# A never-taken branch moved ahead of the second expert pass, and eight modulation steps moved forward at two places of a two-block network

## The chip, the core and the metric

The kernel runs on one core of a Trainium2 chip, in one launch. The metric is device microseconds (us) of that core, the median of the runs shown. The engines are TensorE (PE, matmuls; PEld its weight loads), VectorE (DVE), ScalarE (ACT), GpSimd (POOL) and SyncE (SP), which issues the weight loads. A "q" behind an engine's name is its instruction queue.

## The reference, cut to what matters

Two blocks of two layers each work on 256 tokens of width 1024, all in float32. In the first block a layer is a mixer and a mixture of 16 experts, each behind a norm whose scale and shift come from a small vector `c` through a large matrix; the second block is attention and an MLP, with scales and shifts made in the same way from `c_2` and `c_ctx_2`.

```python
def first_block(x, c, mod_w, mod_b, ...):
    cond = jax.nn.silu(c)
    for layer in range(DEPTH):
        mod = cond @ mod_w[layer] + mod_b[layer]
        sh1, sc1, g1, sh2, sc2, g2 = [m[:, None, :] for m in jnp.split(mod, 6, axis=-1)]
        h = rms_norm(x, mix_norm_g[layer]) * (1 + sc1) + sh1
        ...
        x = x + g1 * mix
        h = rms_norm(x, ffn_norm_g[layer]) * (1 + sc2) + sh2
        ffn = moe(...)
        x = x + g2 * ffn
    return x

def moe(h2, router_w, router_b, w1, w3, w2):
    ...
        y = (jax.nn.silu(xb @ w1[e]) * (xb @ w3[e])) @ w2[e]
        return y * g[:, None]

def second_block(x, c, ctx, c_ctx, w_mod, b_mod, ...):
    for l in range(DEPTH):
        mod = jax.nn.silu(c) @ w_mod[l] + b_mod[l]
        mod_c = jax.nn.silu(c_ctx) @ w_mod[l] + b_mod[l]
        ...
        h = x * (1 + sc1) + sh1
        hc = xc * (1 + sc1c) + sh1c
        y, yc = _token_mixers(h, hc, ...)
        x = _layer_norm(DEEPNORM_ALPHA * x + g1 * y, ln1_g[l], ln1_b[l])
        h = x * (1 + sc2) + sh2
        x = _layer_norm(DEEPNORM_ALPHA * x + g2 * _sq_relu_mlp(h, w_fc1[l], w_fc2[l]), ...)
        ...
```

## The kernel before, in words

`body` runs the phases one after the other: the first mixer (to 200 us), the experts of layer 0 (`moe(0)`, to about 465), the second mixer (`odd_mixer`, to about 583), the experts of layer 1 (to about 866), and block 2, per layer attention (`mixer2`), `out2` and `mlp2`. Activations lie transposed, 128 channels on the partitions by 256 tokens (512 where the context runs along). Weights are float32, split into a high part (`wh`, ScalarE, L332) and a low part (`wl`, VectorE, L325) and multiplied in three products (`linear`, L344 to L346).

**Weights.** `load` (L321) takes the next of a ring of buffers `raw` and issues the transfer from SP's queue. SP works in order: a load whose buffer is still read holds back all that stand behind it. The ring has 11 buffers of 512 KB in the mixers, 9 of 1 MB in the expert stages and 6 of 512 KB in block 2.

**Experts.** `moe` sends the tokens to 16 experts by one-hot products. The experts run in 7 passes over experts with limited room (PASSES: [8..11], [0], [2, 3], [4, 5], [1], [6, 7], [12..15]); `prep` builds a group of passes' inputs (L933) and gates, `up_` multiplies by w1 and w3 (four tiles of 1 MB per expert, L959 into `psab`), applies silu (`sa`, L973), transposes it (L976) and copies it out (`at`, L978); `down` multiplies by w2 (two tiles per expert, L959 into `psY`); `combine` adds the result to `xT` (L1000, L1002). The order of the tiles is up(0), up(1), down(0), up(2), down(1) and so on, 96 tiles per layer.

**Overflow.** Where an expert has more tokens than its room, `overflow` (L797 to L859) computes the rest; its body stands under `tc.If(n > 0)` (L804). With these inputs n is 0, so TensorE, ScalarE, VectorE and GpSimd load n into a register (L802) and branch over the body, about 355 rows of TensorE's program. `new_block` sets a dependency point on ScalarE behind it. Both stand behind `down` of pass 4, ahead of the last pass's `up_`, with the ring filled ahead (`fetch`).

**Modulation steps.** The vectors `mod` are made in groups of 1024 columns: ("a", l, g) for the first block, ("b", l, g) for the second. A group is eight steps (`unit`, L371 to L422): a step loads 128 rows of the matrix (512 KB; in the expert stages two steps share a 1 MB buffer) and multiplies it on TensorE by four products (L406); where `onv` holds an entry when the group begins, VectorE does it in four operations (L391, L393) instead. The eighth step copies the sums, transposes them (L417) and adds the bias (L420). All steps stand in one list, `queue`, in the order of the groups; `fill(n)` issues the next n, `settle` those that finish a group begun, `need` all up to a named group. `fill` does nothing in block 2's attention phases unless told `anyway`. The place of a step in the program is where `fill` stands, and the queue is taken in order, so a `fill` more at one place is a `fill` less later.

**The places around the change.** `odd_mixer` begins with the norm (`norm_split`, L465 to L519) and two linears of eight chunks with a `fill(1)` behind each. `mixer2` of layer 0 begins with the modulation of both streams (`modulate`: `hm`, L1117 or L1115, then its high part `h` on ScalarE, L340, and its low part on VectorE or POOL, L325), and then the chunks `ka`, `qa` with a `fill(1, True)` behind each. In `out2` a `fill(1)` follows each output chunk, and `need` of the groups ("b", 0, 3) and ("b", 0, 4) stands behind the first stream's last; in the first quarter of `mlp2` a step is issued behind a chunk while the queue holds more than 44.

Of the kernel before, what the change touches and what calls it, by code (L numbers as in the profile page):

```python
# [14 lines left out]
AF = mybir.ActivationFunctionType  # L15
# [186 lines left out]
def body(tc, A, out, co, po):  # L202
# [3 lines left out]
    with ExitStack() as ctx:  # L206
# [57 lines left out]
        def Pv(n, a=None, b=None):  # L264
# [10 lines left out]
        sets = {AF.Exp: "natural_log_exp_and_others", AF.Ln: "natural_log_exp_and_others",  # L275
                AF.Silu: "silu_and_others", AF.Sigmoid: "sigmoid_and_others", AF.Tanh: "sigmoid_and_others",
                AF.Gelu_apprx_tanh: "gelu_apprx_tanh_and_others", AF.Sqrt: "sqrt_and_others"}
# [3 lines left out]
        def tables(want):  # L281
            if table["set"] != want:
                before = table["users"] or [table["load"]] * bool(table["load"])
                ld = SC.preload_act_table_set(want)
                tc.keep_in_program_order(ld)
                ld = ld.ins
                for u in before:
                    tc.add_manual_dep(ld, u, nosync, reason="table order")
                table.update(set=want, load=ld.name, users=[])
# [8 lines left out]
        def new_block():  # L298

            t = sm.tile([128, 1], F32, tag="pin", bufs=2, name="pin")  # L300
            table.update(load=SC.copy(t, xT[:, 0, 0:1]).ins.name, users=[])
# [4 lines left out]
        KINDS = {"long": (11, 1024, 4), "wide": (9, 2048, 0), "short": (6, 1024, 3)}  # L306
# [121 lines left out]
        queue, onv = [], []  # L428
# [5 lines left out]
        def fill(n, anyway=False):  # L434
            if "M" not in banks and "ab" not in banks and not anyway:
                return
            for _ in range(min(n, len(queue))):
                queue.pop(0)[1]()
# [422 lines left out]
        def moe(l):  # L861
# [7 lines left out]
            gt, slot, gr, sr, idi, cap, mxc = router(hf, rs, m1(l, 3))  # L869
# [4 lines left out]
            th = [[U(F32R, "th", 4) for _ in range(2)] for _ in range(2)]  # L874
            tl = [[U(F32R, "tl", 4) for _ in range(2)] for _ in range(2)]
# [23 lines left out]
            def fetch(n):  # L899

                while len(ahead) < n:
                    w, r, j = next(todo_w, (None, 0, 0))
                    if w is None:
                        break
                    ahead.append((load(w[l][expert(r), j].rearrange("o p a n -> p (o a n)"), None, 2048), landing[0]))
# [6 lines left out]
            NP = len(PASSES)  # L912
            todo_w = sources()
            wide = lambda p: 128 // len(PASSES[p])
# [50 lines left out]
            def up_(p, pr):  # L965
                xg, _, gs = pr
                oa, ob = ps("ab"), ps("ab")
                for o in (oa, ob):
                    for j in range(2):
                        tiles(p, taken(p), [(o, xg[:, 4 * j + q, :], q * 512, j + q == 0, j + q == 4) for q in range(4)])  # L970
                sa = U(name="sa", bufs=2)
                func(sa, oa, AF.Silu)
                V.scalar_tensor_tensor(sa, sa, gs, ob, op0=OP.mult, op1=OP.mult)  # L973
                o = ps("X")
                for k in range(4):
                    T.transpose(o[:, 128 * k:128 * k + 128], sa[:, 128 * k:128 * k + 128], C("ident"))  # L976
                at = U(name="at", bufs=2)
                V.tensor_copy(at, o)  # L978
                return at
# [26 lines left out]
            for p in range(NP + 1):  # L1006
                if p < NP:
                    at[p] = up_(p, pr[p])
                if p:
                    todo.append((pr[p - 1][1], down(p - 1, at.pop(p - 1))))  # L1010
                    if len(todo) == 2 or p == NP:
                        combine(todo)
                        todo = []
                if groups and GROUPS[groups[0]][0] == p + 2:
                    pr.update(prep(groups.pop(0)))
                if p == NP - 2:
                    fetch(KINDS["wide"][0])
                    tables(sets[AF.Exp])
                    overflow(l, th, tl, gt, slot, cap, mxc)
                    new_block()  # L1020
            tables(sets[AF.Exp])


# [20 lines left out]
            V.tensor_scalar(nclam, clam, -1.0, None, op0=OP.mult)  # L1044

        def odd_mixer():
            assert not any(q[0] in (("a", 1, 0), ("a", 1, 1)) for q in queue)
            hh, hl = Act(8, S, F32R, "hh"), Act(8, S, F32R, "hl")
            norm_split(xT, 1, hh, hl)
            xc, r, ix, u = Act(8, name="xc"), Act(8, name="r"), Act(8, name="ix"), Act(8, name="uu")  # L1050
            y = Act(8, name="sq")
            w = Pv("cv_w").rearrange("p (a b) -> p a b", a=8)
            gw = [[U(name="gw", bufs=4) for _ in range(2)] for _ in range(2)]
            for q in range(2):
                for h in range(2):
                    SY.dma_start(out=gw[q][h].rearrange("p (a b) -> p a b", a=4), in_=A["od_gate"][:, q, 4 * h:4 * h + 4])
            for s in range(8):
                o = ps()
                linear(A["od_in"][8 + s], hh, hl, o[:, :S])
                V.tensor_scalar(xc(s), o[:, :S], w[:, s, 3:4], Pv("cv_b")[:, s:s + 1], op0=OP.mult, op1=OP.add)  # L1060
                for t in range(1, 4):
                    V.scalar_tensor_tensor(xc(s, t), o[:, :S - t], w[:, s, 3 - t:4 - t], xc(s, t), op0=OP.mult, op1=OP.add)
                fill(1)
            for s in range(8):
                o = ps("G")
                c = slice(s % 4 * 128, s % 4 * 128 + 128)
                T.matmul(o[:, :S], lhsT=gw[0][s // 4][:, c], rhs=xc(s), start=True, stop=True)
                T.matmul(o[:, S:], lhsT=gw[1][s // 4][:, c], rhs=xc(s), start=True, stop=True)
                func(r(s), o[:, :S], AF.Sigmoid, bias=Pv("rg_b")[:, s:s + 1])
                func(ix(s), o[:, S:], AF.Sigmoid, bias=Pv("ig_b")[:, s:s + 1])  # L1070
                func(u(s), r(s), AF.Tanh, scale=nclam[:, s:s + 1])
                G.tensor_mul(ix(s), ix(s), xc(s))

            for s in range(8):
                func(r(s), r(s), AF.Exp, scale=clam[:, s:s + 1])
                t = K1("t1")
                func(t, u(s), AF.Ln, bias=1.0)
                func(u(s), u(s), AF.Ln, scale=2.0)
                V.tensor_sub(u(s), u(s), t)
                func(u(s), u(s), AF.Exp, scale=0.5)  # L1080
                G.tensor_mul(ix(s), ix(s), u(s))
                V.tensor_tensor_scan(xc(s), r(s), ix(s), 0.0, op0=OP.mult, op1=OP.add)
            ch, cl = Act(8, S, F32R, "cath"), Act(8, S, F32R, "catl")
            for s in range(8):
                o = ps()
                linear(A["od_in"][s], hh, hl, o[:, :S], 0)
                V.tensor_copy(y(s), o[:, :S])
                fill(1)
            for s in range(8):
                func(y(s), y(s), AF.Gelu_apprx_tanh)  # L1090
                V.tensor_mul(y(s), y(s), xc(s))
                split(ch(s), cl(s), y(s))
            out_proj(A["od_out"], ch, cl, 1)
# [193 lines left out]
        def mixer2(l, bp, hs):  # L1287
# [2 lines left out]
            assert not any(q[0] in (("b", l, 0), ("b", l, 1)) for q in queue)  # L1290
            if l == 0:
                hs = Act(8, 512, F32R, "h", 16, bp), Act(8, 512, F32R, "h", 16, bp)
                for k in range(8):
                    for s in (1, 0):
                        modulate(l, 0, *hs, s, bp, (k,))
# [108 lines left out]

            qn, kn = f"qn{l}", f"kn{l}"
            if l == 0:
                onv.append(1)
                ka = chunk(2, 512)
                qa = [chunk(j, TQ) for j in range(2)]
                vab = values()  # L1410
                kb_ = chunk(5, 512, kn)
                qb_ = [chunk(3 + j, TQ, qn) for j in range(2)]
                settle(True)
                onv.clear()
                attend_ab(qa, ka, 0)
                ckv = low_k()
                cqh, cql = low_q()
                kc = rotary_k()
            else:
                qa = [chunk(j, TQ) for j in range(2)]  # L1420
                qb_ = [chunk(3 + j, TQ, qn) for j in range(2)]
                cqh, cql = low_q()
                ka = chunk(2, 512)
                vab = values()
                kb_ = chunk(5, 512, kn)
                attend_ab(qa, ka, 0)
                ckv = low_k()
                kc = rotary_k()
# [188 lines left out]
```

## Time and profile before

| | |
|---|---|
| median of 3 runs | 1956.85 us (1954.48 to 1958.96) |
| profiled execution | 1955.22 us |
| its span, first to last instruction | 1953.4 us |
| mean granted TensorE clock | 0.959 |
| TensorE busy | 1758.2 us (90%) |
| VectorE busy | 1078.6 us (55%) |
| ScalarE busy | 741.2 us (38%) |
| read from HBM | 437.35 MB |

A busy share is a mean over stages with different limits: in the expert stages the weight stream sets the pace, in block 2 mostly TensorE. A timeline row begins with its start and its length in us; a bracket at its end gives the idle time of the engine before it and what ended it. Windows give the busy time of each engine in a stretch.

### The profile page before, as it was taken

To read this page: it belongs to the slowest core of one execution; us is meant where nothing else is said; L and a number is where in the kernel's file an instruction comes from. 1 tells how busy PE (TensorE), PEld (TensorE's weight loads), DVE (VectorE), ACT (ScalarE), POOL (GpSimd) and SP (SyncE) were. 2 spreads that over 40 slices of the span, in tenths; PEclk is the share of its full clock that TensorE was granted. 3 is DMA by queue.
4 is the path that set the end of the run, shared out by engine and by line. 5 is a ranking of instruction groups with operands and counts; after the bars stand their busy time and mean duration, and the time that the engine had idled before them with its cause. 6 is when DMAs were issued, how large, how long until landed. Compare 5 with 4: busy or idle time off the path is not lost. (4 is left out here: it accounts for less than half of the span.)

```text
span 1953.4 us, 29087 instructions
## 1 busy us (share of the span) xinstructions
PE 1758.2 (90%) x11198; PEld 1256.4 (64%) x11198; DVE 1078.6 (55%) x2298; ACT 741.2 (38%) x1461; POOL 70.7 (4%) x88
## 2 busy tenths in 40 slices
PE   5999689967897799689999999999999999989997
PEld 4866234414783344237655779888888786669996
DVE  4987212104654112048778367678855767666665
ACT  3556100003642000124767355232323656544443
POOL 0000000000200000000010001000000200010000
PEclk8999899978998999889999999999999999989999
DMA  9685999997649999984100675555543220245551
GB/s 378 242 285 193 382 413 419 371 381 311 242 164 369 417 423 380 386 343 156 35 21 33 218 253 188 176 172 187 188 129 130 97 93 22 76 153 182 183 184 44
DMA packets 94361, 440.46 MB, mean 225 GB/s; under 512 B 10240, under 2 KB 10368, under 8 KB 69376
## 3 DMA queue, kind: packets, MB, share of 16 engines
q1 hardware_dynamic: 94208, 438.44, 60.0%
q8 instruction: 93, 1.52, 0.3%
q14 instruction: 60, 0.49, 0.1%
HBM read 437.35 MB, written 1.05 MB: 224 GB/s over the span
## 5 line engine op out<-in xcount | busy, mean ns | idle before, releaser
L332 ACT CAST wh<-raw 128x1024 fp32r<-128x1024 f32 (+1 forms) x258 | 261.4, 1016 | 281.8 <-PE psL L346 209.8
L325 DVE TENSOR_TENSOR wl<-raw,wh 128x1024 fp32r<-128x1024 f32 (+1 forms) x258 | 305.3, 1185 | 97.8 <-ACT wh L332 97.4
L959 PE MATMUL psab<-raw,xg 128*32 128x512 f32 (+2 forms) x1024 | 226.2, 705 | 76.1 <-DMA raw<-w 62.8
L344 PE MATMUL psL<-h,wh 128*128 128x256 f32 (+1 forms) x800 | 258.4, 323 | 7.6 <-ACT h L340 7.6
L345 PE MATMUL psL<-h,wl 128*128 128x256 f32 (+1 forms) x800 | 257.8, 323 | 4.0 <-DVE wl L325 3.9
L346 PE MATMUL psL<-h,wh 128*128 128x256 f32 (+1 forms) x800 | 256.4, 321 | 0.0
L959 PEld LDWEIGHTS psab<-raw,xg 128*32 128x32 f32 (+2 forms) x1024 | 73.9, 147 | 221.7 <-issue 193.7
L344 PE MATMUL psL<-gh,wh 128*128 128x256 f32 (+1 forms) x576 | 185.1, 322 | 0.0
L345 PE MATMUL psL<-gh,wl 128*128 128x256 f32 (+1 forms) x576 | 184.6, 321 | 0.0
L344 PEld LDWEIGHTS psL<-h,wh 128*128 128x128 f32 x800 | 154.2, 193 | 23.4 <-ACT h L340 8.3
L973 DVE SCALAR_TENSOR_TENSOR sa<-sa,gs,psab 128x512 f32<-128x512 f32 x14 | 10.5, 747 | 282.5 <-PE psab L959 282.5
L345 PEld LDWEIGHTS psL<-h,wl 128*128 128x128 f32 x800 | 154.2, 193 | 18.5 <-DVE wl L325 5.1
L346 PEld LDWEIGHTS psL<-h,wh 128*128 128x128 f32 x800 | 153.9, 193 | 14.2 <-issue 4.2
L959 PE MATMUL psY<-raw,at 128*32 128x512 f32 (+2 forms) x512 | 113.1, 611 | 9.3 <-DMA raw<-w 8.4
L346 PE MATMUL psL<-o,wh 128*128 128x256 f32 (+1 forms) x384 | 119.3, 311 | 0.3
L344 PEld LDWEIGHTS psL<-gh,wh 128*128 128x128 f32 x576 | 109.5, 190 | 14.5 <-issue 5.8
L345 PEld LDWEIGHTS psL<-gh,wl 128*128 128x128 f32 x576 | 109.5, 190 | 11.1 <-issue 3.7
L340 ACT CAST yh<-psY 128x512 fp32r<-128x512 f32 x28 | 16.4, 586 | 245.5 <-PE psY L959 245.5
L346 PE MATMUL psL<-gl,wh 128*128 128x256 f32 (+1 forms) x288 | 91.9, 319 | 0.0
L1525 ACT ACTIVATE t<-psL 128x256 f32<-128x256 f32 (+1 forms) x72 | 32.8, 456 | 139.1 <-PE psL L346 139.1
L1123 DVE SCALAR_TENSOR_TENSOR xT<-psL,mod2T,xT 128x256 f32<-128x256 f32 x80 | 38.6, 483 | 84.2 <-PE psL L346 84.0
L344 PE MATMUL psL<-hh,wh 128*128 128x256 f32 x256 | 77.8, 305 | 7.0 <-ACT hh L518 5.5
(449 smaller groups left out, 3340.9 us busy)
## 6 DMA issues: line engine op xcount, KB each, us to landing
raw<-w SPq DMA_DIRECT2D x192, 1024.0 KB, 11.7
raw<-fc SPq DMA_DIRECT2D x144, 512.0 KB, 3.5
raw<-mod_w SPq DMA_DIRECT2D x80, 512.0 KB, 6.6
raw<-w_mod SPq DMA_DIRECT2D x80, 512.0 KB, 3.9
raw<-wo SPq DMA_DIRECT2D x24, 512.0 KB, 4.7
raw<-wi SPq DMA_DIRECT2D x18, 512.0 KB, 3.3
raw<-ev_in SPq DMA_DIRECT2D x16, 512.0 KB, 7.4
raw<-mod_w SPq DMA_DIRECT2D x8, 1024.0 KB, 10.3
```

The costliest lines, as they stand in the source:

```text
L325: eng.tensor_sub(o, a, hi)
L332: SC.copy(hi[:, :w], raw[:, :w])
L340: SC.copy(hi, src)
L344: T.matmul(o, lhsT=wh, rhs=xh, start=start, stop=False)
L345: T.matmul(o, lhsT=wl, rhs=xh, start=False, stop=False)
L346: T.matmul(o, lhsT=wh, rhs=xl, start=False, stop=stop)
L959: r = T.matmul(o[w * i:w * i + w, :], lhsT=x[:, w * i:w * i + w], rhs=loads[i][0][:, c:c + 512], start=first, stop=last)
L973: V.scalar_tensor_tensor(sa, sa, gs, ob, op0=OP.mult, op1=OP.mult)
L1123: V.scalar_tensor_tensor(src2[s][:, n, :], o[:, s * S:s * S + S], mod2T[l][:, g, s, n:n + 1], src2[s][:, n, :], op0=OP.mult, op1=OP.add)
L1525: SC.activation(t[:, a:b], o[:, a:b], AF.Relu)
```

## The change

The block of `fetch`, `overflow` and `new_block` moves from behind pass 4 (`p == NP - 2`) to behind the `up_` of the first pass, in both expert stages. `odd_mixer` begins with `fill(8)`. `mixer2` of layer 0 issues eight steps ahead of the modulation, and the entry that puts the next group on VectorE goes in there too instead of ahead of `ka`. Nothing that is computed changes; the list of steps is only taken up earlier by eight at each of the two places.

```diff
@@ -1006,6 +1006,11 @@
             for p in range(NP + 1):
                 if p < NP:
                     at[p] = up_(p, pr[p])
+                if p == 0:
+                    fetch(KINDS["wide"][0])
+                    tables(sets[AF.Exp])
+                    overflow(l, th, tl, gt, slot, cap, mxc)
+                    new_block()
                 if p:
                     todo.append((pr[p - 1][1], down(p - 1, at.pop(p - 1))))
                     if len(todo) == 2 or p == NP:
@@ -1013,11 +1018,6 @@
                         todo = []
                 if groups and GROUPS[groups[0]][0] == p + 2:
                     pr.update(prep(groups.pop(0)))
-                if p == NP - 2:
-                    fetch(KINDS["wide"][0])
-                    tables(sets[AF.Exp])
-                    overflow(l, th, tl, gt, slot, cap, mxc)
-                    new_block()
             tables(sets[AF.Exp])
 
 
@@ -1044,6 +1044,7 @@
             V.tensor_scalar(nclam, clam, -1.0, None, op0=OP.mult)
 
         def odd_mixer():
+            fill(8)
             assert not any(q[0] in (("a", 1, 0), ("a", 1, 1)) for q in queue)
             hh, hl = Act(8, S, F32R, "hh"), Act(8, S, F32R, "hl")
             norm_split(xT, 1, hh, hl)
@@ -1290,6 +1291,8 @@
             assert not any(q[0] in (("b", l, 0), ("b", l, 1)) for q in queue)
             if l == 0:
                 hs = Act(8, 512, F32R, "h", 16, bp), Act(8, 512, F32R, "h", 16, bp)
+                fill(8, True)
+                onv.append(1)
                 for k in range(8):
                     for s in (1, 0):
                         modulate(l, 0, *hs, s, bp, (k,))
@@ -1404,7 +1407,6 @@
 
             qn, kn = f"qn{l}", f"kn{l}"
             if l == 0:
-                onv.append(1)
                 ka = chunk(2, 512)
                 qa = [chunk(j, TQ) for j in range(2)]
                 vab = values()
```

On TensorE the first pass and what follows it stand so in layer 0 before (psab<-raw,xg are products of `up_`, psX<-cst_108,sa the transposes of its result, psX<-P,th the preparation L933):

```order
774 L802 ISA x2
775 L959 MATMUL psab<-raw,xg 32x512 x64
776 L959 MATMUL psab<-raw,xg 128x512 x2
777 L976 MATMUL psX<-cst_108,sa 128x128 x4
778 L933 MATMUL psX<-P,th 128x256 x2
```

Behind the last of these stand the rest of the preparation, 14 more products of the second pass and the first down products. Now the branch follows the transposes, with the skipped body behind it:

```order
774 L802 ISA x2
775 L959 MATMUL psab<-raw,xg 32x512 x64
776 L976 MATMUL psX<-cst_108,sa 128x128 x4
777 L804 COMPARE_AND_BRANCH
778 L814 MATMUL psX<-cst_108,oP 128x128
```

Behind the body's end (row 1132) stand the 32 products L933, and then:

```order
1149 L941 MATMUL psX<-cst_108,P 128x128 x2
1150 L944 MATMUL psX<-rt,P 128x2 x2
1151 L941 MATMUL psX<-cst_108,P 128x128 x2
1152 L944 MATMUL psX<-rt,P 128x2 x2
1153 L959 MATMUL psab<-raw,xg 128x512 x16
1154 L959 MATMUL psY<-raw,at 32x512 x4
1155 L976 MATMUL psX<-cst_108,sa 128x128 x4
1156 L959 MATMUL psY<-raw,at 32x512 x28
```

All 16 products of the second pass stand behind the preparation, also the two that stood ahead of the transposes, and the branch stands between the transposes and the preparation. At the old place the compare and the body are gone.

On VectorE block 2 begins so before (hm and h are the modulation's, wl the low part of a weight, p the steps that VectorE does):

```order
883 L1117 TENSOR_SCALAR hm<-cT,mod2T_85 128x256
884 L1117 TENSOR_SCALAR hm<-xT,mod2T_85 128x256
885 L325 TENSOR_TENSOR wl<-raw,wh 128x1024
886 L325 TENSOR_TENSOR h<-hm,h 128x256 x2
887 L1117 TENSOR_SCALAR hm<-cT,mod2T_85 128x256
888 L1117 TENSOR_SCALAR hm<-xT,mod2T_85 128x256
889 L391 TENSOR_SCALAR p<-raw,cond_93 128x512 x2
890 L1117 TENSOR_SCALAR hm<-cT,mod2T_85 128x256
891 L1117 TENSOR_SCALAR hm<-xT,mod2T_85 128x256
892 L391 TENSOR_SCALAR p<-raw,cond_93 128x512
893 L325 TENSOR_TENSOR h<-hm,h 128x256 x2
894 L391 TENSOR_SCALAR p<-raw,cond_93 128x512
```

and now so (the lines of the changed kernel count one higher here):

```order
896 L1118 TENSOR_SCALAR hm<-cT,mod2T_85 128x256
897 L1118 TENSOR_SCALAR hm<-xT,mod2T_85 128x256
898 L1118 TENSOR_SCALAR hm<-cT,mod2T_85 128x256
899 L1118 TENSOR_SCALAR hm<-xT,mod2T_85 128x256
900 L325 TENSOR_TENSOR h<-hm,h 128x256 x2
901 L420 TENSOR_TENSOR mod2T_85<-psO,pv 128x8 x2
902 L325 TENSOR_TENSOR wl<-raw,wh 128x1024
903 L391 TENSOR_SCALAR p<-raw,cond_93 128x512 x4
904 L325 TENSOR_TENSOR wl<-raw,wh 128x1024
905 L393 SCALAR_TENSOR_TENSOR p<-raw,cond_93,p 128x512 x4
```

Ahead of these rows stand eleven more rows of hm and h alone: the whole chain of the modulation is now ahead of the first split and of the first step on VectorE, which stood among it.

On SP's queue block 2 begins so before (wi are the weights of the chunks, w_mod the steps'):

```order
537 L256 DMA cst<-cst 128x1536
538 L321 DMA raw<-wi 128x1024
539 L321 DMA raw<-w_mod 128x1024
540 L321 DMA raw<-wi 128x1024
541 L321 DMA raw<-w_mod 128x1024
542 L321 DMA raw<-wi 128x1024
```

and now so:

```order
538 L256 DMA cst<-cst 128x1536
539 L321 DMA raw<-w_mod 128x1024 x8
540 L321 DMA raw<-wi 128x1024
541 L321 DMA raw<-w_mod 128x1024
542 L321 DMA raw<-wi 128x1024
543 L321 DMA raw<-w_mod 128x1024
```

Eight loads of steps stand ahead of the first weight. In `odd_mixer`, likewise, eight loads raw<-mod_w stand ahead of those of the gates' weights (gw). In `out2` the run of nine loads raw<-w_mod ahead of one wo is gone, single loads alternate with wo.

## Rows read from the trace of the kernel before

**Rows 1.** The line of cores of the profiled execution.

```profile
core 0: 1953.4 us, clock 0.959
```

**Rows 2.** Windows: engines' busy us, PEclk, DMA share, GB/s; both expert stages.

```profile
275.00:280.00 5.00, 4.95 (x44) 1.74 (x36) 0.26 (x1) 0.60 (x2) 0.00 (x0) 1.00 0.88 305
...
390.00:395.00 5.00, 4.25 (x10) 1.52 (x8) 0.79 (x2) 1.28 (x3) 0.00 (x0) 1.00 1.01 421
...
400.00:405.00 5.00, 3.86 (x20) 1.25 (x24) 0.00 (x0) 1.48 (x2) 0.00 (x0) 0.50 0.82 339
405.00:410.00 5.00, 5.00 (x44) 1.51 (x40) 0.00 (x0) 0.00 (x0) 0.00 (x0) 0.83 0.28 79
...
805.00:810.00 5.00, 5.00 (x44) 1.45 (x40) 0.00 (x0) 0.00 (x0) 0.00 (x0) 0.90 0.23 59
```

**Rows 3.** Timeline of TensorE behind the branch's old place, layer 0: start, length, instructions.

```profile
401.14 9.37 PE L959 MATMUL psab<-raw,xg 128*32 128x512 f32 x60 [6.89 <-DVEq L804]
```

**Rows 4.** Instructions of line L804: ns min/median/max, first and last start.

```profile
L804 PEldq COMPARE_BRANCH  x2: 5812/5880/5949, 387.8 to 790.0; - x2
...
L804 DVEq COMPARE_BRANCH  x2: 63/68/72, 395.5 to 797.5; - x2
...
L804 DVEq EVENT_SEMAPHORE  x2: 21/21/21, 401.0 to 802.8; - x2
```

**Rows 5.** Timeline of TensorE around the new place, layer 0.

```profile
246.24 7.23 PE L959 MATMUL psab<-raw,xg 128*32 128x512 f32 x36 [4.67 <-DMA raw<-w]
...
253.66 0.48 PE L933 MATMUL psX<-P,th 128*128 128x256 f32 x2
...
258.78 12.26 PE L959 MATMUL psab<-raw,xg 128*128 128x512 f32 x28
...
272.55 7.40 PE L959 MATMUL psY<-raw,at 128*32 128x512 f32 x64
283.20 8.78 PE L959 MATMUL psab<-raw,xg 128*64 128x512 f32 x32 [3.25 <-DMA raw<-w]
```

**Rows 6.** Timeline of VectorE at the new place.

```profile
253.95 0.69 DVE L978 COPY at<-psX 128x512 f32<-128x512 f32 x1 [1.41 <-PE psX L976]
```

**Rows 7.** Windows at the second mixer's start, columns as in group 2.

```profile
460.00:465.00 5.00, 4.77 (x30) 2.02 (x21) 2.15 (x5) 2.46 (x3) 0.00 (x0) 0.87 0.00 0
...
480.00:485.00 5.00, 5.00 (x26) 5.00 (x25) 4.22 (x7) 1.84 (x3) 0.00 (x0) 0.50 1.02 419
```

**Rows 8.** Timeline of TensorE in the second mixer's first linear.

```profile
479.23 0.58 PE L345 MATMUL psL<-hh,wl 128*128 128x256 f32 x1 [1.32 <-DVE wl L325]
```

**Rows 9.** Timeline of VectorE at the start of block 2.

```profile
867.04 1.22 DVE L325 TENSOR_TENSOR wl<-raw,wh 128x1024 fp32r<-128x1024 f32 x1
```

**Rows 10.** Timeline of POOL there: the chain's last pair.

```profile
884.11 2.29 POOL L325 TENSOR_TENSOR h<-hm,h 128x256 fp32r<-128x256 f32 x2 [3.04 <-ACT h L340]
```

**Rows 11.** Timeline of TensorE there: the third chunk begins.

```profile
888.40 0.39 PE L344 MATMUL psS<-h,wh 128*128 128x512 f32 x1
888.63 0.39 PE L345 MATMUL psS<-h,wl 128*128 128x512 f32 x1
```

**Rows 12.** Windows behind it, columns as in group 2 (VectorE is the third).

```profile
900.00:910.00 10.00, 10.00 (x69) 9.24 (x68) 10.00 (x15) 3.12 (x5) 0.00 (x0) 1.00 0.75 243
910.00:930.00 20.00, 20.00 (x93) 14.18 (x91) 14.54 (x26) 11.34 (x18) 0.00 (x0) 1.00 0.35 118
```

**Rows 13.** Timeline of TensorE in out2: four modulation steps in a row.

```profile
1110.33 1.93 PE L406 MATMUL psM<-raw,cond2r 128*32 128x256 f32 x32
```

**Rows 14.** Timeline of SP's queue in out2.

```profile
1096.34 15.48 SPq L321 DMA_DIRECT2D raw<-w_mod  x9
```

**Rows 15.** Waits, 1065 to 1215 us: total us, times, longest.

```profile
ACT wh L332 <- DMA raw<-wo: 17.1, 6, 5.1
```

**Rows 16.** Windows in out2, columns as in group 2 (TensorE is the first).

```profile
1120.00:1125.00 5.00, 3.97 (x28) 3.27 (x27) 4.40 (x12) 3.99 (x8) 0.00 (x0) 1.00 1.01 391
1125.00:1130.00 5.00, 3.50 (x33) 2.33 (x33) 5.00 (x11) 4.51 (x9) 0.00 (x0) 1.00 0.78 257
```

## The prediction

> **What bounds the kernel now.** I read the line of cores first [rows 1]: span 1953.4 us, mean granted clock 0.959. The profiled execution took 1955.22 us, so 1.8 us lie around the span, and it stands 1.6 us under the median of the three runs, 1956.85. Every sum below is made against 1955.22; the 1.6 is added at the end. A measurement of this kernel can tell about 0.2%, 3.9 us, from no change.
>
> Next I read stretches of five microseconds around the old place of the branch, for DMA rate and clock. In the expert stages the weight stream runs at some 421 GB/s (390 to 395 us) [rows 2], and the layer ends when its 96 tiles of 1 MB are through and used, so a hole in this stream is lost unless TensorE was the later one anyway. Behind the branch there is such a hole in each layer: 339 GB/s and then 79 in layer 0, 59 in layer 1. TensorE's timeline shows why: the last pass's products (p = 6, experts 12 to 15) start at 401.14 after 6.89 us in which it waited for VectorE's queue at L804 [rows 3]. The rows of line L804 [rows 4] give the length of the skipped branch: VectorE's compare stands at 395.5 and the event that ends the region at 401.0; TensorE's own branch takes 5812 to 5949 ns.
>
> Then I read TensorE and VectorE at the new place [rows 5, 6], and last the places where the modulation steps are moved [rows 7 to 16].
>
> **Part 1: the branch moves ahead of the second pass.** What goes away: 5 x (1 - 339/421) + 5 x (1 - 79/421) = 1.0 + 4.1 = 5.1 us of stream in layer 0, and 5 x (1 - 59/421) = 4.3 us in layer 1 [rows 2], 9.4 us in all. The old TensorE stall was longer, 6.9 us, but nine loaded tiles stood ahead of it, and only what the stream lost counts.
>
> What comes instead: the order shows TensorE branching right behind the four transposes of the first pass, and VectorE right behind the copy of their result, with preparation of passes 2 and 3 (L933) behind. That copy ends at 253.95 + 0.69 = 254.64 [rows 6]. From compare to event VectorE took 5.5 us at the old place [rows 4]; with the compare at the end of that copy the event comes near 260.1, and L933, which now starts at 253.66 [rows 5], starts 6.5 us later. The two first products of the second pass, four records, filled the wait for the transposes before; now they follow the preparation: 4 x 12.26/28 = 1.75 us later [rows 5]. Against that, the transposes no longer stand behind them, about 0.75 us. After a pause of six microseconds the clock stood at 0.50 at the old place (400 to 405 us) [rows 2], and the next stretch had 0.83, so up to 2.7 us of work was lost; I take 2.0, since the preparation's short products need not all scale. That is 6.5 + 1.75 - 0.75 + 2.0 = 9.5 us.
>
> What could hide it is the wait for data on either side: TensorE waits 4.67 us for a tile before this place and 3.25 us after it, before the third pass at 283.20 [rows 5]. I do not count these as cover, because the ring has nine tiles: the tiles of the third pass go into the places that the first down products (272.55) release, and the DMA share falls to 0.88 at 275 to 280, with 305 GB/s [rows 2]. The stream is waiting for those releases already; a later release makes the third pass later by the same amount. Only the loss already there, 5 x (1 - 305/421) = 1.4 us, is not paid a second time. So 8.1 us per layer, 16.2 in two (layer 1 has the same order), and **part 1 is 16.2 - 9.4 = +6.8 us**. Its bounds are 0 per layer (all hidden in the two waits, -9.4 in all) and 9.5 (+9.6). I take the value near the upper one because of the ring, and for what I expect keep +2 to +9.6.
>
> [...]
>
> **Part 2: eight steps ahead of the second mixer's norm.** Each step is a 512 KB load and four products L406. In the order their loads stand ahead of the gate weights, where the DMA moves nothing (460 to 465 us, 0 GB/s) [rows 7]; 4 MB at 421 GB/s are 10 us and fit from where the experts' last tiles release their places. Their 32 products, 2 x 1.93 = 3.9 us by [rows 13], fall where TensorE waits for the norm. VectorE's order puts the eight pairs of the norm ahead of the first weight split, which now stands among them, so the first product L345 comes near 482.4 instead of 479.23 [rows 8], 3.2 us later. But TensorE ran at 0.50 from 480 to 485 [rows 7], after a pause that the 32 products now fill: at full clock 2.9 us from 482.4 do what was done by 485.2. **Part 2 is +0.5 us**; bounds +3.2 (clock as low as before) and -2 (first product no later, clock full).
>
> **Part 3: eight steps at the start of block 2.** Eight loads stand ahead of the first weight, 32 products ahead of the first linear on TensorE, and VectorE does the whole chain of `hm` and `h` before its first weight split. Before, that split was at 867.04 [rows 9] and the chain's last pair left POOL at 884.11 + 2.29 = 886.4 [rows 10]; both first chunks were through at 888.40, where the third starts [rows 11]. VectorE's part of the chain gets shorter without splits and steps: three splits of 1.22 us [rows 9] are 3.7 us of its time, and the steps L391 and L393 stood among them too; I give the chain 4.4 us, so that it ends near 882. With a split of 1.22 the first chunk runs from 883.3, 24 products, and the second, 24 more, behind it. One product follows the other in 0.23 us (888.40, 888.63) [rows 11], so both end near 894.4: 6 us later. VectorE's steps that were done among the chain now fall where it is full (10.00 of 10 us in 900 to 910) [rows 12], with 5.5 us free in 910 to 930; I add 1.5. **Part 3 is +7.5 us**; bounds +1 (the chain alone ends both) and +11 (chain no faster, more waits for splits).
>
> **Part 4: what is then missing later.** The queue is eight ahead after the mixer's norm and sixteen by block 2's second norm: 16 steps fewer in `out2` and the first quarter of `mlp2`. By [rows 13] four units are 1.93 us, so 16 are 7.7 us of TensorE. That engine is the bound there: in the two weakest stretches it is still busy 3.97 + 3.50 of 10 us [rows 16]. A run of nine loads stands ahead of an output weight in SP's queue there (15.48 us) [rows 14], ScalarE waits 17.1 us in six times for such weights [rows 15], and TensorE's 2.5 idle us of the two stretches come behind that run. I count 2.3 as saved. **Part 4 is -10 us**; bounds -12 and, where the waits stay and something else fills the gap, -2. What follows has the same steps as before.
>
> **Sum:** 6.8 + 0.5 + 7.5 - 10 = +4.8 us, 1960.0 for the profiled execution, 1961.6 on the median.
>
> **The rivals**, with times on the median. (a) *The pause is hidden at the new place*, which ends on the other side: TensorE waits 4.67 and 3.25 us for tiles there [rows 5], 7.9 in all, and if the stream is ahead by the length of the pause nothing is late. Part 1 is then -9.4, the sum -11.4, 1945. It decides from a cost under 3.8 us per layer, where the sum passes -3.9. For it speaks that these are true waits for data; against it the share of 0.88 at 275. Chance 0.12. (b) *The new start of block 2 hides behind the chain*: part 3 is +1, the sum -1.7, 1955. For it: VectorE is full in this stretch, and loses its splits and steps; against it, the one split now behind the chain. Chance 0.18. (c) *The branch costs the same in both places*, 4.7 us per layer: part 1 is 0, the sum -2.0, 1955. Chance 0.10. (d) *The relief doesn't arrive*: `out2` waits for weights and splits as before, part 4 is -2, the sum +12.8, 1970. Chance 0.15.
>
> **How the numbers follow.** My forecast has the remaining 0.45, by itself 1957 to 1966. Of it 0.02 is faster, 0.18 within 0.2% and 0.25 slower. (a) is faster, (b) and (c) give 0.11 faster and 0.17 within, (d) is slower with small rests: faster 0.25, same 0.33, slower 0.42. The range reaches from 1947, just over (a), to 1970, which takes in (d).
>
> **What would show it.** Part 1: no hole at 405; VectorE's event near 260 in layer 0; L933 a good six microseconds later; the third pass eight later. If the third pass starts under 287, (a) holds. Part 2: first L345 of the mixer 3 us later against the end of the experts, at full clock. Part 3: its third chunk 6 us or more later against the end of the experts; 1 us means (b). Part 4: that delay made good and 2 to 3 us more by 1220 us. A time under 1950 makes part 1 wrong, one over 1966 part 4.

## The result, and the profile after

The changed kernel takes 1974.26 us (median of 4 runs, 1971.96 to 1975.53) beside 1957.9 for the kernel before: ratio 1.0085, interval 1.0067 to 1.0102, so 16.6 us slower (13.1 to 20.0). The prediction had the sign, with +4.8 us, and a range that ended at 1970.

The line of cores of the profiled execution (1975.53 us) answers to [rows 1]:

```profile
core 0: 1973.8 us, clock 0.952
```

Windows of the changed kernel, columns as in [rows 2]. The first four lie behind the branch's new place in layer 0, the next two at the old place, the last two at the second mixer's start (they answer to [rows 7]):

```profile
255.00:260.00 5.00, 1.19 (x4) 1.14 (x5) 0.00 (x0) 0.19 (x1) 0.00 (x0) 0.52 1.01 421
260.00:265.00 5.00, 2.19 (x11) 2.19 (x11) 0.69 (x1) 0.00 (x0) 0.00 (x0) 0.50 1.00 415
265.00:270.00 5.00, 5.00 (x32) 5.00 (x31) 0.69 (x1) 1.52 (x3) 0.00 (x0) 0.62 0.22 90
270.00:275.00 5.00, 5.00 (x14) 2.35 (x14) 1.52 (x12) 1.66 (x2) 0.00 (x0) 1.00 0.16 23
405.00:410.00 5.00, 3.41 (x32) 0.78 (x24) 1.02 (x2) 0.46 (x1) 0.00 (x0) 1.00 1.01 426
410.00:415.00 5.00, 1.11 (x8) 0.45 (x12) 0.00 (x0) 0.00 (x0) 0.00 (x0) 0.72 1.02 433
480.00:485.00 5.00, 1.53 (x5) 1.21 (x5) 3.64 (x11) 3.93 (x8) 0.00 (x0) 0.55 1.02 419
485.00:490.00 5.00, 3.81 (x18) 3.81 (x19) 2.27 (x2) 2.08 (x3) 0.00 (x0) 0.50 0.89 329
```

The hole at the old place is gone: 426 and 433 GB/s. A larger one stands behind the new place, 90 and 23 GB/s: the ring's nine tiles were loaded, and SP waited for the products that free one, 21.0 us at the longest (waits from 255 to 290 us):

```profile
SPq L321 <- PE psab L959: 29.0, 4, 21.0
```

TensorE's timeline there (beside [rows 5]; left out are the transposes and the rest of the 32 products L933) shows why:

```profile
245.26 5.15 PE L959 MATMUL psab<-raw,xg 128*32 128x512 f32 x32 [4.86 <-DMA raw<-w]
...
258.19 0.76 PE L933 MATMUL psX<-P,th 128*128 128x256 f32 x2 [6.09 <-DVEq L804]
258.76 0.63 PE L933 MATMUL psX<-P,tl 128*128 128x256 f32 x2
262.81 0.59 PE L933 MATMUL psX<-P,th 128*128 128x256 f32 x2 [3.42 <-issue]
263.20 0.63 PE L933 MATMUL psX<-P,tl 128*128 128x256 f32 x2
263.62 0.63 PE L933 MATMUL psX<-P,th 128*128 128x256 f32 x2
...
269.99 13.98 PE L959 MATMUL psab<-raw,xg 128*128 128x512 f32 x32
...
293.40 3.65 PE L959 MATMUL psab<-raw,xg 128*64 128x512 f32 x16 [1.68 <-DMA raw<-w]
```

The pause of the branch is 6.09 us, close to the 6.5 of the forecast. But after four records (products, as the trace holds them) TensorE stands idle again, for 3.42 us, and for nothing the profile shows ("issue"). The rest of the preparation runs at the half clock (0.50, then 0.62 in the windows): one pair of products follows the other in 0.43 us, where it was 0.24 us in the kernel before. The third pass starts at 293.40. Two rows of the kernel before, for the pace:

```profile
254.22 0.40 PE L933 MATMUL psX<-P,th 128*128 128x256 f32 x2
254.46 0.40 PE L933 MATMUL psX<-P,tl 128*128 128x256 f32 x2
```

The waits of TensorE over the whole program sum this up (what waits <- for what: us, times, longest):

```profile
PE psX L933 <- DVEq L804: 12.2, 2, 6.1
...
PE psM L417 <- ACT mod_e L414: 8.0, 5, 5.6
...
PE psX L933 <- issue: 6.1, 2, 3.4
...
PE psO L417 <- ACT k L414: 5.6, 1, 5.6
```

The second idle stretch comes in both layers. And TensorE now waits twice for 5.6 us ahead of L417, once in each of the places that got eight steps.

From the timelines I read where the time went, with one profiled execution of each kernel: the expert stages run from the first product of `up_` to the end of the last of `down`, "between" lies between the two stages, "rest" behind the second. A second execution of the changed kernel differs by up to 2.6 us in a column, and layer 1 of the five kernels with the branch at its old place reads 242.3 to 245.7, so differences under some 3 us say nothing.

| kernel | layer 0 | between | layer 1 | rest | measured against before, us |
|---|---|---|---|---|---|
| before | 245.9 | 156.8 | 242.3 | 1091.4 | |
| the change | 250.5 | 161.8 | 253.0 | 1092.5 | +16.6 (13.1 to 20.0) |
| the change again | 251.4 | 162.5 | 250.4 | 1093.1 | +15.9 (11.0 to 20.8) |
| branch only | 251.5 | 156.9 | 246.4 | 1094.8 | +8.4 (4.9 to 11.8) |
| mixer steps only | 246.0 | 163.7 | 245.7 | 1087.4 | -3.7 (-6.5 to -1.0) |
| block 2 steps only | 245.2 | 157.6 | 245.2 | 1097.9 | +3.7 (1.0 to 6.7) |
| both steps | 245.5 | 162.6 | 243.7 | 1091.5 | +1.0 (-1.4 to 3.3) |
| no branch at all | 239.0 | 155.3 | 242.1 | 1092.0 | -4.5 (-7.8 to -1.4) |
| branch behind preparation | 246.1 | 155.7 | 246.5 | 1095.8 | +6.7 (3.9 to 9.4) |
| branch ahead of first pass | 235.4 | 163.5 | 233.8 | 1093.3 | -7.4 (-10.0 to -4.7) |
| the change, shifted by 8 products | 246.3 | 163.6 | 247.1 | 1095.4 | +11.0 (7.6 to 14.3) |
| mixer steps behind the gates | 244.0 | 171.9 | 243.4 | 1088.1 | +7.3 (4.5 to 10.0) |
| branch first, eight mixer steps | 235.8 | 166.7 | 236.1 | 1087.3 | -6.7 (-9.2 to -4.1) |
| branch first, four mixer steps | 236.4 | 173.2 | 236.4 | 1090.0 | -5.1 (-8.4 to -1.8) |

The last column is the measured ratio times the median of the kernel before in the same comparison (1957.9 to 1961.6). The profiled executions are single ones: those of before (1955.22) and without a branch (1949.07) lie 3 to 6 us below their medians, those of the mixer steps alone (1962.96) and of the last row (1961.14) 5 us above, so a row's sum and its last column differ.

### The profile page after: what moved, and what is told of

Same layout as the page of the kernel before. It is cut to its first block, busy times and chain, and to the rows that moved or that the text cites. A ratio compares the mean times of both kernels' runs of the same rounds, so it can differ in the third digit from the quotient of the medians.

```text
span 1973.8 us, 29087 instructions
## 1 busy us (share of the span) xinstructions
PE 1764.1 (89%) x11198; PEld 1261.1 (64%) x11198; DVE 1080.6 (55%) x2298; ACT 741.6 (38%) x1461; POOL 68.8 (3%) x88
## 3 DMA queue, kind: packets, MB, share of 16 engines
q8 instruction: 94, 1.54, 0.3%
## 5 line engine op out<-in xcount | busy, mean ns | idle before, releaser
L344 PE MATMUL psL<-h,wh 128*128 128x256 f32 (+1 forms) x800 | 256.9, 321 | 7.6 <-ACT h L340 7.6
L345 PE MATMUL psL<-h,wl 128*128 128x256 f32 (+1 forms) x800 | 257.7, 323 | 3.9 <-DVE wl L325 3.8
L344 PE MATMUL psL<-gh,wh 128*128 128x256 f32 (+1 forms) x576 | 185.1, 322 | 0.0
L345 PE MATMUL psL<-gh,wl 128*128 128x256 f32 (+1 forms) x576 | 184.6, 321 | 0.0
L344 PEld LDWEIGHTS psL<-h,wh 128*128 128x128 f32 x800 | 153.5, 192 | 22.4 <-ACT h L340 8.3
L345 PEld LDWEIGHTS psL<-h,wl 128*128 128x128 f32 x800 | 153.3, 192 | 20.1 <-issue 6.2
L973 DVE SCALAR_TENSOR_TENSOR sa<-sa,gs,psab 128x512 f32<-128x512 f32 x14 | 10.5, 748 | 277.2 <-PE psab L959 277.2
L344 PEld LDWEIGHTS psL<-gh,wh 128*128 128x128 f32 x576 | 109.5, 190 | 14.5 <-issue 5.8
L345 PEld LDWEIGHTS psL<-gh,wl 128*128 128x128 f32 x576 | 109.5, 190 | 11.2 <-issue 3.7
L393 DVE SCALAR_TENSOR_TENSOR sq<-raw,cond,sq 128x512 f32<-128x512 f32 x112 | 77.6, 746 | 11.1 <-DMA raw<-w_mod 11.1
L959 PEld LDWEIGHTS psY<-raw,at 128*32 128x32 f32 (+2 forms) x512 | 35.2, 132 | 72.3 <-issue 59.9
```

The costliest lines, as they stand in the source:

```text
L344: T.matmul(o, lhsT=wh, rhs=xh, start=start, stop=False)
L345: T.matmul(o, lhsT=wl, rhs=xh, start=False, stop=False)
L393: V.scalar_tensor_tensor(a, w, cols[1][:, i, k:k + 1], a, op0=OP.mult, op1=OP.add)
L959: r = T.matmul(o[w * i:w * i + w, :], lhsT=x[:, w * i:w * i + w], rhs=loads[i][0][:, c:c + 512], start=first, stop=last)
```

## The experiments

**The change taken apart.** Four kernels that each hold some hunks of the change's diff: the branch's move alone (its first two), `odd_mixer`'s alone (the third), block 2's alone (the last two), and both step moves.

```diff
+            fill(8)
...
+                fill(8, True)
+                onv.append(1)
...
-                onv.append(1)
```

> The kernel before with the branch alone moved behind the first pass's up products, in both layers; no step is moved. Theory A (the branch carries the loss: its pause is followed by an idle stretch of 2.6 to 3.4 us of TensorE for its own program and by products at half clock, and the stream's ring can't cover it): 13 to 16 us slower than before. Theory B (the branch costs what the prediction said, +6.8 us, and the moved steps carry the rest): 5 to 8 us slower.

> The kernel before with the eight steps ahead of the second mixer's norm alone. Theory A: the mixer's start is 3.4 us later and out2 has eight steps fewer, 3.9 us of TensorE: between -1 and +3 us. Theory B: +4 to +6 us.

> The kernel before with the eight steps at block 2's start alone. Theory A: the start is some 8 us later, eight steps fewer afterwards and no run of nine loads give 4 to 7 back: +1 to +4 us. Theory B: +4 to +6 us.

> Both step moves, the branch at its old place. Theory A: 1 to 5 us slower, and with the branch-only run it adds up to the 16 us of the whole change. Theory B: 9 to 11 us slower.

Measured +8.4, -3.7, +3.7 and +1.0 us. The branch alone lay between the two theories, with an interval (4.9 to 11.8) that takes in all of B; the steps spoke for A at block 2's start and together, and the mixer's steps alone came out below both. But +8.4 and +1.0 make 9.4, not 16: the pieces don't add up. The table shows where: in layer 1, 246.4 with the branch alone and 253.0 with everything. In the branch-only run TensorE's second idle stretch was there in one layer of two:

```profile
PE psX L933 <- DVEq L804: 12.5, 2, 6.3
PE psX L933 <- issue: 3.5, 1, 3.5
```

**Is it the place in the program?** Its timeline in layer 1 has no such stretch, and the products return to full pace after 4 us. Between the layers, the mixer's steps add 64 records of L406 and their weight loads to TensorE's program. So the next four kernels were the change again, no branch at all, and the branch at two other places.

> The changed kernel once more, beside the three below. Theory A (branch and steps add up, and the first measurement stands high): +9 to +11 us, as the branch alone (+8.4) and the steps alone (+1.0) make. Theory C (they don't add up: TensorE's second idle stretch behind the branch comes in both layers of the whole change and in one layer of the branch alone, and the moved steps shift TensorE's program between the two layers): +14 to +19 us, and the trace shows an idle stretch without a releaser behind the branch in both layers.

The ratio was 1.0081 (1.0056 to 1.0106), and the idle stretch came in both layers again (5.4 us in two times), behind the same number of records, 4 in layer 0 and 10 in layer 1. So the change costs more than its pieces; how much more is uncertain (by the intervals, an estimate, 2 to 12 us).

```diff
-                    overflow(l, th, tl, gt, slot, cap, mxc)
-                    new_block()
```

> The kernel before with the overflow left out altogether (with these inputs it is never entered), nothing else moved: the price of the old place. By the prediction's reading, the holes in the stream behind it are its price: 8 to 10 us faster. If the holes are made good later, 0 to 4 us faster.

The kernel without the branch was 4.5 us faster (1.4 to 7.8): the old place cost about half of what its holes in the stream, 9.4 us, had promised. In the traces most of it lies in layer 0, 239.0 us beside 244.0 to 246.0 in the five kernels with the branch at its old place; layer 1 has 242.1 beside 242.3 to 245.7.

```diff
-                if p == NP - 2:
+                if p == 0:
                     fetch(KINDS["wide"][0])
```

> The branch stands one place later than in the change: behind the preparation of passes 2 and 3, ahead of the second pass's products; no step is moved. Theory A (pause, idle stretch and half clock on the 32 short products make the loss): the preparation runs at full clock ahead of the branch, what follows are long products that need few instructions, no idle stretch: +2 to +5 us against before, 4 to 6 less than the branch alone. If the pause itself is the whole loss: as the branch alone, +7 to +10.

+6.7 us (3.9 to 9.4): between the two cases, and its interval reaches into both, so it doesn't tell them apart. It does show that, with the preparation done ahead and no idle stretch of 3 us behind, the pause (13.4 us in two times) still has a price, and the measured one is most of what the branch alone costs.

```diff
             for p in range(NP + 1):
+                if p == 0:
+                    fetch(KINDS["wide"][0])
+                    tables(sets[AF.Exp])
+                    overflow(l, th, tl, gt, slot, cap, mxc)
+                    new_block()
                 if p < NP:
```

> The branch stands ahead of the first pass's products; no step is moved. There TensorE waits for four groups of tiles, 16 us in sum, since the stream has only begun. Theory A (the place decides by what the stream has ahead): the pause delays the first release, the ring's nine tiles last until then, and the stream loses 0 to 3 us per layer instead of 4.7: -9 to -3 us against before. If a pause costs its full length anywhere (6 us per layer): +2 to +4.

-7.4 us. The same pause stands there, 6.94 us in layer 0:

```profile
222.04 3.59 PE L959 MATMUL psab<-raw,xg 128*32 128x512 f32 x11 [6.94 <-DVEq L804]
```

The stage begins some 5 us later, but is 10.5 and 8.5 us shorter: 235.4 and 233.8 us. The stream has only begun, and TensorE would have waited for tiles there anyway (from 215 to 260 us 16.0 us in four times before, 8.7 us in two here): in layer 0 the preparation L933 begins at 255.27, only 1.6 us later than before (253.66). With the branch here the kernel is no slower than without any (-4.5, intervals overlap).

**Eight products that do nothing.** At the very start of the whole change:

```diff
+                spare_o = ps("X")
+                for _ in range(8):
+                    T.matmul(spare_o[:, 0:1], lhsT=ones, rhs=ones[:, 0:1], start=True, stop=True)
```

> The whole change, with eight one-column products on TensorE put at the program's very start, 32 instructions, whose result nothing reads. They cost nothing there (TensorE waits for its first data) and shift everything behind by 32 places in TensorE's program. Theory C (the idle stretch behind the branch is TensorE waiting for the next piece of its program, which begins a few instructions behind the branch's end: after 4 products in layer 0, after 10 in layer 1): the shift puts the branch's end behind the start of that piece, the idle stretch is gone in both layers, the second pass starts 4 to 6 us earlier in each, and the whole is +4 to +10 us against before instead of +16. If the idle stretch has another cause (semaphores, data, the clock): it stays, and the time too, +14 to +19.

The idle stretch is gone in both layers, in the waits (no line L933 <- issue is left) and in the timeline of layer 0:

```profile
260.13 0.77 PE L933 MATMUL psX<-P,th 128*128 128x256 f32 x2 [6.39 <-DVEq L804]
260.69 0.63 PE L933 MATMUL psX<-P,tl 128*128 128x256 f32 x2
261.12 0.63 PE L933 MATMUL psX<-P,th 128*128 128x256 f32 x2
```

The order of all other products on TensorE is the same in the two traces, so the shift is what differs. The kernel takes 1971.11 us, 1.0056 (1.0039 to 1.0073), that is +11.0 us: some 5 of the 16 us came from where the branch's end falls in TensorE's program (by the intervals, an estimate, 1 to 10 us). Layer 0 is 246.3 instead of 250.5 and 251.4, layer 1 247.1 instead of 253.0 and 250.4. The second pass starts 4.5 us earlier in layer 0, as forecast, but in layer 1 only 2.6 and 0.8 us earlier than in the two executions of the change, where the transposes ahead of it also came 1.7 us later; the total came out just above the forecast of +4 to +10. From the first L933 to the second pass TensorE took 6.7 us here in layer 0 and 7.5 in layer 1, beside 11.8 and 11.5 (10.7 and 9.7 the second time) in the change:

```profile
266.87 13.98 PE L959 MATMUL psab<-raw,xg 128*128 128x512 f32 x32
```

**The mixer's steps at another place**, between the gates and the second linears of the same mixer:

```diff
+            fill(8)
             ch, cl = Act(8, S, F32R, "cath"), Act(8, S, F32R, "catl")
```

> The kernel before with the second mixer's eight steps at another place of the same mixer: behind the gates, ahead of its second linears, where TensorE stood idle for some 6 us; the branch and block 2's start are as before. If the steps' cost in the change is the mixer's later start (its first weights stand behind eight loads): the stretch between the two expert stages is 156 to 159 us in the trace instead of 162 to 164, and the kernel is 3 to 8 us faster than before. If eight steps cost the same wherever they stand in the mixer: as at its start, 162 and a total like that of the steps at its start alone (-3.7).

A miss: +7.3 us (4.5 to 10.0), with 171.9 us between the stages. TensorE's timeline names the reason:

```profile
530.15 1.02 PE L417 MATMUL psM<-cst,mod_e 128*128 128x8 f32 x4 [11.99 <-ACT mod_e L414]
```

The transposes of a group's end stand in TensorE's order ahead of the linears, and their input is copied by ScalarE, whose order has the copy behind a long chain. In the kernel before, products of these linears fill that time, from

```profile
510.83 0.47 PE L344 MATMUL psL<-hh,wh 128*128 128x256 f32 x1
```

on. Eight steps cost some 3.7 us of products (64 records L406), but where they end a group they tie TensorE to ScalarE's queue, here for 11.99 us.

**Combinations.** The branch ahead of the first pass, with eight and with four steps ahead of the mixer's norm (the two edits shown above, the second in its form for four):

```diff
         def odd_mixer():
+            fill(4)
```

> Two pieces that were faster alone: the branch ahead of the first pass (-7.4) and the eight steps ahead of the second mixer's norm (-3.7); block 2's start as before. If they add up: -14 to -8 us. If the moved program brings an idle stretch behind the branch here too, or the mixer's late start adds to the pause: -7 to 0.

> The branch ahead of the first pass, and four steps (not eight) ahead of the second mixer's norm: half a group, so that its transposes L417, which wait for ScalarE's copy behind the whole norm, no longer stand ahead of the first linear on TensorE. If that wait is what makes the mixer late (6 us with eight steps): the first L344 comes 10 to 12 us after the experts' last product instead of 16, the stretch between the expert stages is 2 to 4 us shorter than with eight steps (166.7 in that trace), and the total is -11 to -7 against before. If the loads ahead of the first weights make it late: the first L344 at 13, half of the delay, and a total like that of the branch ahead of the first pass with eight steps (-6.6) or without (-7.4).

With eight steps -6.7 us (-9.2 to -4.1), with four -5.1 (-8.4 to -1.8): nothing is gained beyond the branch's place. With four, "between" is 173.2 us, longer than the 166.7 with eight where 2 to 4 us less were expected; TensorE waits 8.37 us for a weight split within the second linears. The four-step kernel also refutes half of my reason. No L417 stands ahead of its first linear, and still the first L344 came 15.8 us after the experts' last product, because (first row; the second is the wait of 8.37)

```profile
478.50 0.58 PE L344 MATMUL psL<-hh,wh 128*128 128x256 f32 x1 [6.61 <-ACT wh L332]
...
533.78 0.58 PE L344 MATMUL psL<-hh,wh 128*128 128x256 f32 x1 [8.37 <-ACT wh L332]
```

ScalarE's first weight split stands behind all eight `hh` of the norm (476.61 is the last). In the kernel before, the first split (473.89) stood ahead of all `hh`. It is the order that ScalarE got with the steps ahead that delays the mixer, with or without the transposes.

The lowest ratio seen is that of the branch ahead of the first pass with no step moved: 1951.49 us (12 runs), 0.9962 (0.9949 to 0.9976). The interval of the eight-step kernel overlaps it.

## Why the prediction was wrong

Of the 11.8 us between the forecast of +4.8 and the measured +16.6, 8.8 lie in part 1 and 3.0 in the other parts: the change is 15.6 us slower than the two step moves alone (+16.6 and +1.0), where part 1 had +6.8, and the step moves made +1.0 (-1.4 to 3.3), where parts 2 to 4 had -2.0.

- **Part 1, what comes instead: a term was missing.** The step "+6.5 + 1.75 - 0.75 + 2.0" held in its first three terms: measured from the stage's start, L933 begins 5.6 us later (258.19 - 215.97 against 253.66 - 217.00), the transposes 0.8 us earlier, and the products behind take 1.7 us more. What failed is that the sum let TensorE run on at once behind the pause and so put any further idle time at nothing. From L933's start to the second pass it took 11.8 us instead of 5.1: 3.42 us of idle stretch that no row of the kernel before shows, and 3.3 us of half clock (pairs of products 0.43 us apart, not 0.24) instead of 2.0. The third pass then began 11.2 us later in layer 0 (77.4 us after the stage's start instead of 66.2) and 12.6 in layer 1, not 8.1; in the second execution of the change 10.9 and 9.8. Where the stretch is missing, the sum held: 1.6 to 2.3 us of half clock, and a third pass 7.4 and 9.0 us late in the shifted kernel and 6.6 in layer 1 of the branch alone.
- **Part 1, what goes away: over-sized.** 9.4 us of holes were counted as lost time; leaving the branch out brought 4.5. Why the rest of the holes was made good was not tested. With both corrections part 1 is 11.2 + 12.6 - 4.5 = 19.3 us, with the second execution 16.2, beside the 15.6 above.
- **Part 1, the reading of the ring held**: the waits for tiles on either side did not cover the pause, the stream stood still (90 and 23 GB/s), and rival (a) fell with the third pass at 293.40.
- **Part 2: a wrong step.** "A pause that the 32 products now fill": the products, 64 records, began at 474.11, then TensorE waited 5.58 us for ScalarE's copy, and the clock was 0.55 and 0.50 from 480 to 490, when the linear began, as it had been (0.50) from 475 to 485 before. The first L345 came at 486.19, 16.8 us after the experts' last product (L1000) instead of 13.4: 3.4 us later, as the sum had it for VectorE. But the gain at full clock never came, and "between" is 5 to 7 us longer (161.8 to 163.7) in every kernel with these steps at this place and the branch not ahead of the first pass, instead of 0.5. That the mixer's steps alone still measured -3.7, near the -4.5 of part 2 and half of part 4, is luck as far as the traces show: "rest" is 4 us shorter, and where the remainder came back stays open.
- **Part 3: right in size; part 4 somewhat over-sized.** The third chunk starts at 916.11, 31.9 us after the last L1000 instead of 23.5, 8.4 us late (predicted 6, and 7.5 with what follows). The "rest" is 1.1 and 1.7 us longer where -2.5 was expected, so the sixteen steps that are missing later gave back some 7 us, not 10. Block 2's steps alone cost 3.7 us.
- The sum's sign was right, and its range was too short at the upper end: a pause after which the engine doesn't run at once was in no rival. The prediction would have put a time over 1966 down to part 4; it was mostly part 1.

The rows of the changed kernel that part 2 is read from:

```profile
474.11 3.66 PE L406 MATMUL psM<-raw,cond1r 128*32 128x256 f32 x64
483.35 1.02 PE L417 MATMUL psM<-cst,mod_e 128*128 128x8 f32 x4 [5.58 <-ACT mod_e L414]
486.19 0.58 PE L345 MATMUL psL<-hh,wl 128*128 128x256 f32 x1 [1.31 <-DVE wl L325]
```

TensorE's branch takes 5.81 to 6.32 us in both layers of the kernel before, the change (two executions), the branch alone, the branch behind the preparation, the branch ahead of the first pass and the shifted kernel (rows of L804). Over the whole execution of the changed kernel the transfers by queue count 94 instruction packets, 1.54 MB. In the idle stretch, 260 to 261 us, they show one of 0.02 MB beside the weights (for which engine the view doesn't say):

```profile
q1 hardware_dynamic: 55, 0.39, 93.1%
q8 instruction: 1, 0.02, 5.6%
```

In the shifted kernel such a packet comes too, at 262 to 263 us, but there TensorE is busy with L933, which began at 260.13:

```profile
q8 instruction: 1, 0.02, 6.0%
```

So the packet alone proves nothing. That the changed kernel had run out of instructions when it came, and waited for it, is my inference, which no view shows; that the place in TensorE's program decides is shown by the eight products (idle stretches of 3.42 and 2.64 us without them, none with them).

## What to carry to other kernels

What the pause cost went by its place here: against the kernel before, the branch alone made +8.4 us behind the first pass's products, +6.7 behind the preparation (the intervals overlap) and -7.4 ahead of the first pass, and leaving it out made -4.5; it cost nothing measurable where TensorE was still waiting for the stage's first tiles. So ask what each engine does in the ten microseconds behind a pause, and whether the stream has tiles and free buffers until then. When a branch or any block of code moves, test it at two or three program positions (a few instructions more ahead of it); otherwise an accident of place, some 5 us here, is taken for the change's worth. Work that filled one engine's gap was not free here, where its last step waited for another engine's queue (TensorE for ScalarE's copy, 5.58 us at the mixer's start and 11.99 us behind the gates): see what stands behind it in that engine's order.

## What the runs showed of the hardware that was not expected

A never-taken branch over some 355 rows of TensorE's program took TensorE 5.81 to 6.32 us at its four places, and the work behind it began when VectorE's own branch had ended too (in the changed kernel the event at 258.0, L933 at 258.19), after a pause of 5.9 to 7.3 us. In one of these places up to 3.49 us of idle time followed, depending on where the branch's end falls in the program: 4 records behind it in layer 0, 10 in layer 1, none when the program was shifted by eight products. After the pause alone the products at that place ran at half clock for another 3.5 to 5.3 us (pairs of L933 0.43 us apart instead of 0.24; the granted clock was 0.50 from 665 to 670 us in the branch-only run). Beside the kernel without it, the same branch cost between some 13 us (the branch alone, +8.4 against -4.5) and nothing measurable (ahead of the first pass, -7.4 against -4.5). Two kernels whose pieces measured +8.4 and +1.0 made +16 together. In the traces the one piece shifted the other's program, and the second idle stretch came with it; the shifted kernel, with no stretch at all, still stands at +11.0, so this explains a part of the gap and not surely all of it.
